# The inverse's working block and the state sum of a chunked scan, moved from SBUF to PSUM

## The chip, the cores and the metric

The kernel runs as one program on one core of a Trainium2 chip. The metric is the device time of one execution in microseconds (us). Three runs of the kernel before took 4306.79, 4306.83 and 4312.45 us; their median is 4306.83 us. The engines are named as in the profile: PE is the tensor engine (PEld its weight loads), DVE the vector engine, ACT the scalar engine, POOL the GpSimd engine, SP the engine that issues most of the DMAs.

## The reference

The model has two layers over 1024 latent tokens with 256 context tokens ahead of them, width 1024, in float32. Layer 0 mixes tokens with attention and a convolution; layer 1 mixes them with a bidirectional RWKV-7 scan; each layer ends in a SwiGLU feed-forward block. The change lies in the scan of layer 1:

```python
def step(S, inp):
    w_t, k_t, v_t, kk_t, b_t = inp[:5]
    sa = jnp.einsum('bhvk,bhk->bhv', S, kk_t)
    S = S * w_t[:, :, None, :] - sa[..., None] * b_t[:, :, None, :] + v_t[..., None] * k_t[:, :, None, :]
    y = jnp.einsum('bhvk,bhk->bhv', S, inp[5]) if emit else None
    return S, y
```

It runs for 16 heads of 64 features, forward and backward, first over the context and then, from the state so reached, over the latent tokens.

## The kernel before

**Stages.** The program goes through layer 0, the projections of layer 1, the scan (`layer1_scan`, lines 987 to 1407), and then the output projection and the feed-forward block of layer 1, which is nearly all matmuls. The scan lies between about 2400 and 3430 us of the span.

**The scan by chunks.** Tokens are cut into chunks of 64. The heads are done in four quarters `Q` of four heads, and each quarter in five scan steps `g` (the context, then four windows of 256 tokens), so there are 20 scan steps. A scan step handles both directions at once, four chunks each. Inside a chunk the recurrence is a triangular system, and its inverse is worked out ahead, on the chip. Four generators make up the work of a scan step, and the loop at the end of `layer1_scan` advances them in turn: `scan` of step n, `prep_inv` and `prep_mat` of step n+1, `prep_in` of step n+2.

**The inverse (`prep_inv`).** The 32 by 32 diagonal blocks lie in `A` with one half block per partition; `X` (128 partitions by 32 rows by 16 columns, 2 KB per partition) starts as a constant pattern `xid` and becomes the inverse by forward substitution. For each of 31 rows `k` there are two DVE instructions: line 1203 multiplies a column of `A` by row `k` of `X` into `tmp`, line 1204 subtracts `tmp` from the remaining rows of `X`. With n = 31-k rows and a width of k//2+1, the 31 rows hold 2856 elements per partition. Then `X` is transposed twice on DVE (lines 1207 and 1209, into `xd` and `xt`), ACT copies the result into `xc` (line 1214), and PE forms the off-diagonal block in two rounds of 32 small matmuls each per half (lines 1221 and 1228), each round into a PSUM tile `gp` that ACT reads out (lines 1224 and 1230). Both `gp` tiles come from the PSUM pool `pg`, which has one buffer of one bank (2 KB per partition) under the tag "g".

**The scan of a chunk (`scan`).** PE adds the values' part and the old state's part into `px` (lines 1263 and 1265), ACT copies it (1267), PE applies the inverse (1270, `pu`), ACT copies it (1272), PE forms the state's increment `ps` (line 1277, `pss` in the profile), DVE adds the old state `sc` (line 1284, `t` in the profile) and multiplies by the decay (line 1286, the new `sc`). `px`, `pu` and `pss` of a direction share one PSUM bank, under the tag c0 or c1, so each of them waits until the one before it has been read. POOL does the elementwise products of the preparation, all through line 1056 (`pmul`).

**Order.** The kernel is written in a tile framework, which places the waits and decides, with a timing model of its own, the fixed order of the instructions on each engine. [...] A tile's buffer is taken again only when all readers and writers of the tile that had it are done.

Of the kernel before, what the change touches and what calls it, by code (L numbers as in the profile page):

```python
# [9 lines left out]
F32 = mybir.dt.float32  # L10
F32R = mybir.dt.float32r
AF = mybir.ActivationFunctionType
# [31 lines left out]
class Kern:  # L44
# [7 lines left out]
    # ---------------------------------------------------------------- helpers  # L52
# [10 lines left out]
    def load_w(self, src, k=KB, m=P):  # L63
        """weight block (k*128 rows, m columns of DRAM) -> exact high and low parts"""
        raw = (self.Wr or self.W).tile([P, KB, P], F32, tag="raw", name="raw", bufs=self.wraw)
        if self.Wr:
            self.next_w()
        hi = self.W.tile([P, KB, P], F32R, tag="whi", name="whi", bufs=self.wbuf)
        lo = self.W.tile([P, KB, P], F32R, tag="wlo", name="wlo", bufs=self.wbuf)
        r, h, l = raw[:, :k, :m], hi[:, :k, :m], lo[:, :k, :m]  # L70
        self.nc.sync.dma_start(r, src.rearrange("(k p) m -> p k m", p=P))
        self.split(h, l, r)
        return h, l

    def load_w_rows(self, src):
        """128 rows by up to 1024 columns -> high and low parts"""
        n = src.shape[1]
        raw = (self.Wr or self.W).tile([P, KB, P], F32, tag="raw", name="raw", bufs=self.wraw)
        if self.Wr:
            self.next_w()  # L80
        hi = self.W.tile([P, KB, P], F32R, tag="whi", name="whi", bufs=self.wbuf)
        lo = self.W.tile([P, KB, P], F32R, tag="wlo", name="wlo", bufs=self.wbuf)
        fl = lambda t: t.rearrange("p a b -> p (a b)")[:, :n]
        self.nc.sync.dma_start(fl(raw), src)
        self.split(fl(hi), fl(lo), fl(raw))
        return fl(hi), fl(lo)

    # -------------------------------------------------------------- constants
# [19 lines left out]
    def params(self, *groups):  # L108
        """small parameters, a block of 128 features per column"""
# [40 lines left out]
    def ada(self, l, g0, g1, pool, bufs, psA, psT):  # L150
        """modulation of layer l for both condition vectors, groups g0..g1 of 1024 features: one step per weight block"""
        nc = self.nc
        for g in range(g0, g1):
            pa = psA.tile([P, 512], F32, tag="o", name="ada")[:, :256]
            for kb in range(KB):
                raw = pool.tile([P, D], F32, tag="araw", name="araw", bufs=bufs)
                nc.sync.dma_start(raw, self.I["ada_w"][l][kb * P:(kb + 1) * P, g * D:(g + 1) * D])
                for j in range(4):
                    nc.tensor.matmul(pa[32 * j:32 * j + 32], self.silc[:, kb], raw[:, 256 * j:256 * j + 256], start=kb == 0, stop=kb == KB - 1)
                if kb == KB - 1:  # L160
                    rows = pool.tile([P, 256], F32, tag="adr", name="adr", bufs=1)
                    nc.vector.tensor_copy(rows, pa)
                    pt = psT.tile([P, 512], F32, tag="o" if psA is psT else "m", name="adt")
                    for q in range(2):
                        nc.tensor.transpose(pt[:, q * P:(q + 1) * P], rows[:, q * P:(q + 1) * P], self.ident)
                    o = self.mod[l][:, g * 8:g * 8 + 8].rearrange("p (j q) s -> p j q s", q=2)
                    b = self.par["ada_b"][:, l * 48 + g * 8:l * 48 + g * 8 + 8].rearrange("p (j q) -> p j q", q=2)
                    nc.vector.tensor_tensor(o, pt[:, 0:256].rearrange("p (q j x) -> p j q x", q=2, j=4)[:, :, :, 0:2],
                                            b[:, :, :, None].to_broadcast([P, 4, 2, 2]), op=ALU.add)
                yield  # L170
# [8 lines left out]
    def rstd_bcast(self, src, n, scale, eps, pool, psum, tag="nn", bufs=3):  # L179
        """1/sqrt(scale * (sums of src over its blocks and their rows) + eps), on every partition: PSUM [P, n]"""  # L180
# [15 lines left out]
    def norm_mod(self, h, l, which, pool, psum):  # L196
        """h [P, 8, n] -> generator of (token range, fb, t, shift) with t = h * gain * rstd"""
# [26 lines left out]
    def load_hT(self, t0, n, dst, pool, psum, xb=4):  # L224
        """tokens t0..t0+n of the input streams, transposed: dst [P, 8, n]"""
# [17 lines left out]
    # ------------------------------------------------------- layer 0: mixer  # L243
    def layer0_mix(self):
# [6 lines left out]
        with ExitStack() as st:  # L251
# [96 lines left out]
            def conv(j, c=0, n=L - 30):  # L348
                """depthwise convolution of channel block j from column c on, to DRAM"""
# [8 lines left out]
            def conv2(j, cs):  # L358
                """the same, with the products and the sums on the other engines"""
# [17 lines left out]
            with tc.tile_pool(name="T1", bufs=1, side="right", reuse_waits="tile") as tp:  # L377
# [28 lines left out]
                # rotated keys, the same for all heads, by token  # L406
# [17 lines left out]
            # rotations with the gains of the rotated features; gains of the others, by feature  # L424
# [29 lines left out]
            def pair(p, wp, wn):  # L454
                """queries, keys (by token, normalised and rotated) and values of heads 2p and 2p+1"""
# [57 lines left out]
            # what is done with first lies where the residual stream comes next  # L513
            E = pool(left, name="AE", bufs=1)
            N = pool(left, name="AT", bufs=1)
            # what ends first lies where the loads of the next phase come
            N2 = pool(left, name="AH", bufs=1)
            vts[1] = values(N, 1)
            # queries and keys by feature, with a row for the maximum
# [6 lines left out]
            def head(i):  # L526
                """queries and keys of a head by feature"""
# [16 lines left out]
            def maxima(i):  # L544
                """maxima of the scores, as one more feature of the queries"""
# [19 lines left out]
            def attend(i):  # L565
# [3 lines left out]
                for t0, n in TT[1:] + TT[:1]:  # L569
# [16 lines left out]
                    # the other half of the rows holds the sums, the same in every row  # L586
# [15 lines left out]
            def conv_norm(t0):  # L602
                """layer norm over the channels, up to the shift, of 256 tokens, in place in DRAM"""
# [17 lines left out]
            def spread(gen, n, a, b):  # L621
                """n steps of gen between steps a and b of the attention of a head"""
                return [gen, n, a, b, 0]
# [39 lines left out]
    def layer0_out(self, hT, xh, xl, psum, tp):  # L663
        """the mixer's output projection; and the normalised input of the ffn"""
# [15 lines left out]
    def mix_out(self, l, wsrc, hT, xh, xl, passes, kbs, psum, rest, early=()):  # L680
        """residual stream plus gated projection; then the normalised input of the ffn, but for the last pass"""
        nc = self.nc
        self.gains(l, 1)
        # passes of (block of features, token tiles); the early ones have their weights, and most products, already
# [32 lines left out]
    # ------------------------------------------------------------------- ffn  # L717
# [46 lines left out]
    # ------------------------------------------------- layer 1: projections  # L764
    def layer1_proj(self, hT, close_h, LR):
# [8 lines left out]
        # lora features by direction, high parts in the direction's own rows, low parts in the others  # L774
# [8 lines left out]
        with ExitStack() as st:  # L783
# [10 lines left out]
            # heads of a feature block: sums over them, and back to their features  # L794
# [21 lines left out]
            def next_w():  # L816
                """the weight blocks rotate through two pools"""
# [4 lines left out]
            def mixed(o, i, fb, t0, n=256):  # L822
                """token mix i of feature block fb"""
# [162 lines left out]
    # ------------------------------------------------- layer 1: chunked scan  # L986
    def layer1_scan(self, R, prepared):
# [5 lines left out]
        with ExitStack() as st:  # L993
# [8 lines left out]
            # constants  # L1002
# [23 lines left out]
            # which keys a query sees, by token of the key: removal keys (lower rows) and keys (upper rows)  # L1026
# [17 lines left out]
            # tiles with parts that stay  # L1044
# [32 lines left out]
            def prep_in(Q, q, g, n):  # L1077
                """decayed keys and queries of the chunks of scan step g (both directions)"""
# [3 lines left out]
                for d, u in enumerate(units):  # L1082
# [21 lines left out]
                    # running sum of sigmoid(decay) in each chunk; products of decays and their inverses  # L1104
# [31 lines left out]
                for d, u in enumerate(units):  # L1136
                    # products of the removal keys with their queries, and the 32 by 32 diagonal blocks
# [20 lines left out]
            def prep_mat(Q, q, g, units):  # L1158
                """products of the chunks' keys with their queries, and the keys by token"""
# [32 lines left out]
            def prep_inv(units, par):  # L1192
                """inverses of the triangular systems of the chunks, transposed"""
                dt = units[0].dt
                # inverses of the diagonal blocks: one block per partition, its columns shared by two
                X = S.tile([P, 32, 16], F32, tag="X", name="X", bufs=1)
                nc.gpsimd.tensor_scalar(X, xid, 1.0, 0.0, op0=ALU.mult, op1=ALU.add)
# [12 lines left out]
                # inverses of the 64 by 64 blocks, transposed  # L1210
# [26 lines left out]
            def load_v(Q, tok, d):  # L1237
                """values of two chunks, in the upper rows"""
# [11 lines left out]
            def scan(Q, q, g, units):  # L1250
                lat = g > 0
                for j in range(4):
                    for d in range(2):
# [19 lines left out]
                        if not (g == 4 and j == 3):  # L1273
# [9 lines left out]
                            t1 = U.tile([P, 2, 64], F32, tag=f"t1{d}", name="t1", bufs=2)  # L1283
                            nc.vector.tensor_tensor(t1, ps, sc, op=ALU.add)
                            scn = U.tile([P, 2, 64], F32, tag=f"sc{d}", name="sc", bufs=3)
                            nc.vector.tensor_tensor(scn, t1, u.pc[:, :, m:m + 1].to_broadcast([P, 2, 64]), op=ALU.mult)
# [122 lines left out]
    def layer1_in(self, xh, xl, tp):  # L1409
        """the mixer's output, but for the last quarter of the features"""  # L1410
# [26 lines left out]
    # --------------------------------------------------------------------- all  # L1437
    def run(self):
        tc = self.tc
        pool = lambda s, **k: s.enter_context(tc.tile_pool(reuse_waits="tile", **k))  # L1440
        with ExitStack() as st:
# [12 lines left out]
            def phase(l, sizes, x, out):  # L1454
                """output projection of a mixer and the ffn after it; residual stream in hT"""
# [114 lines left out]
```

## Time and profile before

| | |
|---|---|
| median of three runs | 4306.83 us |
| span of the profiled execution, first to last instruction | 4304.2 us |
| PE busy | 3881.8 us (90%) |
| DVE busy | 2617.4 us (61%) |
| ACT busy | 1728.2 us (40%) |
| POOL busy | 1167.9 us (27%) |
| lines 1203 and 1204 together, DVE | 541.7 us in 1240 instructions |

A row of the profile names the line, the engine, the operation, the tiles (output <- inputs), the shapes and the count; behind the bar stand the total busy time in us and the mean of one instruction in ns, and then the time for which the engine idled just before them, with what ended most of it. A row of the timeline begins with the start in us and the length in us. A row of busy time by window gives the window, its length, and then for each engine the busy time and the number of instructions, and after those the granted clock of PE as a share of full speed, the share of the DMA engines and GB/s.

### The profile page before, as it was taken

The page shows a single profiled execution, that of the slowest core. Times are in us where ns is not written, and L with a number is a line of the kernel's source. Part 1 is how long each engine was busy: PE and PEld are TensorE (multiplying, and loading weights), DVE is VectorE, ACT ScalarE, POOL GpSimd, SP SyncE. Part 2 cuts the span into 40 slices and gives each one's busy share as a digit, 9 for nine tenths or more (in the row PEclk, how much of TensorE's full clock was granted, in tenths as well). Part 3 has the DMA queues.
Part 4 walks back from the last instruction along what each step waited for, and adds up shares of the span by engine and source line. Part 5 has one row for each costly group of instructions (what it writes and reads, how often), then busy time and mean ns, then how long its engine had stood idle before and what let it go on. Part 6 is the DMA issues. An engine that isn't in the chain of part 4 may idle for free. (4 is left out here: it accounts for less than half of the span.)

```text
span 4304.2 us, 70559 instructions
## 1 busy us (share of the span) xinstructions
PE 3881.8 (90%) x28764; PEld 3171.4 (74%) x28764; DVE 2617.4 (61%) x4577; ACT 1728.2 (40%) x3568; POOL 1167.9 (27%) x998
## 2 busy tenths in 40 slices
PE   8887999899999999979999578777877899999999
PEld 5665666688888888868779556666665778888887
DVE  5698676554343333366775798998899754333333
ACT  4436666632111111145665355556555533111111
POOL 3869455310000000042231443445344210000000
PEclk9898999899999999989999878787887899999999
DMA  4422221421111111022322211222222141111111
GB/s 169 138 68 74 85 85 61 152 69 45 35 40 40 40 40 40 30 79 69 112 89 87 75 56 49 73 67 64 70 65 63 52 126 59 49 49 47 42 49 59
DMA packets 301668, 297.06 MB, mean 69 GB/s; under 512 B 19408, under 2 KB 267872, under 8 KB 301344
## 3 DMA queue, kind: packets, MB, share of 16 engines
q1 hardware_dynamic: 293488, 277.07, 20.5%
q10 hardware_dynamic: 7056, 14.75, 1.0%
q8 instruction: 227, 3.72, 0.4%
q0 software_dynamic: 800, 0.73, 0.1%
q14 instruction: 97, 0.79, 0.1%
HBM read 246.36 MB, written 46.14 MB: 68 GB/s over the span
## 5 line engine op out<-in xcount | busy, mean ns | idle before, releaser
L59 PE MATMUL pf<-xh,whi 128*128 128x512 f32 (+1 forms) x1760 | 654.4, 372 | 0.0
L61 PE MATMUL pf<-xh,wlo 128*128 128x512 f32 (+1 forms) x1760 | 654.2, 372 | 0.0
L60 PE MATMUL pf<-xl,whi 128*128 128x512 f32 (+1 forms) x1760 | 654.0, 372 | 0.0
L54 ACT ACTIVATE whi<-raw 128x1024 fp32r<-128x1024 f32 (+1 forms) x207 | 214.8, 1048 | 905.3 <-PE pf L60 788.6
L762 DVE SCALAR_TENSOR_TENSOR hT<-pf,mod,hT 128x512 f32<-128x512 f32 (+1 forms) x440 | 306.0, 697 | 196.5 <-PE pf L61 194.5
L55 DVE TENSOR_TENSOR wlo<-raw,whi 128x1024 fp32r<-128x1024 f32 (+1 forms) x207 | 268.9, 1309 | 254.1 <-ACT whi L54 249.1
L751 DVE TENSOR_TENSOR sl<-sl,pf 128x512 f32<-128x512 f32 (+1 forms) x110 | 69.7, 634 | 580.9 <-PE pf L61 580.9
L60 PEld LDWEIGHTS pf<-xl,whi 128*128 128x128 f32 x1760 | 331.0, 188 | 64.6
L59 PEld LDWEIGHTS pf<-xh,whi 128*128 128x128 f32 x1760 | 330.9, 188 | 64.7 <-ACT xh L221 0.3
L61 PEld LDWEIGHTS pf<-xh,wlo 128*128 128x128 f32 x1760 | 330.8, 188 | 64.5
L60 PE MATMUL pf<-gl,whi 128*128 128x512 f32 (+1 forms) x880 | 324.1, 368 | 0.0
L61 PE MATMUL pf<-gh,wlo 128*128 128x512 f32 (+1 forms) x880 | 323.9, 368 | 0.0
L59 PE MATMUL pf<-gh,whi 128*128 128x512 f32 (+1 forms) x880 | 323.9, 368 | 0.0
L1204 DVE TENSOR_TENSOR X<-X,tmp 128x126 f32<-128x126 f32 (+22 forms) x620 | 274.3, 442 | 13.3
L581 POOL TENSOR_TENSOR pl<-pe,pt 128x512 fp32r<-128x512 f32 (+1 forms) x176 | 226.9, 1300 | 190.2 <-PE po L60 104.8
L1203 DVE TENSOR_TENSOR tmp<-A,X 128x126 f32<-128x126 f32 (+22 forms) x620 | 267.4, 431 | 13.3
L791 POOL MEMSET apad<- 128x8 f32 x4 | 0.2, 122 | 884.7 <-PE pf L61 884.7
L367 POOL TENSOR_TENSOR co<-co,cpr 128x655 f32<-128x655 f32 x90 | 193.7, 2153 | 46.0 <-ACT cpr L366 36.7
L54 ACT ACTIVATE gh<-sl 128x512 fp32r<-128x512 f32 (+1 forms) x110 | 64.9, 590 | 307.5 <-DVE sl L751 307.5
L59 PEld LDWEIGHTS pf<-gh,whi 128*128 128x128 f32 x880 | 165.9, 189 | 27.8
L60 PEld LDWEIGHTS pf<-gl,whi 128*128 128x128 f32 x880 | 165.9, 189 | 27.7
L61 PEld LDWEIGHTS pf<-gh,wlo 128*128 128x128 f32 x880 | 165.9, 189 | 27.7
(407 smaller groups left out, 9763.9 us busy)
## 6 DMA issues: line engine op xcount, KB each, us to landing
raw<-in_ffn_w_dram SPq DMA_DIRECT2D x132, 512.0 KB, 3.8
araw<-in_ada_w_dram SPq DMA_DIRECT2D x96, 512.0 KB, 4.4
low<-lod SPq DMA_DIRECT2D x40, 256.0 KB, 2.7
kw<-kd SPq DMA_DIRECT2D x40, 256.0 KB, 2.8
kkw<-kkd SPq DMA_DIRECT2D x40, 256.0 KB, 2.8
sv<-vd SPq DMA_DIRECT2D x80, 128.0 KB, 2.9
raw<-in_even_w_out_dram SPq DMA_DIRECT2D x16, 512.0 KB, 3.7
rw<-rd SPq DMA_DIRECT2D x32, 256.0 KB, 3.0
```

Of the source, the lines that this page charges most:

```text
L54: self.nc.scalar.activation(hi, src, AF.Copy)
L55: return self.nc.vector.tensor_tensor(lo, src, f32(hi), op=ALU.subtract)
L59: mm(ps, wh, xh, start=start, stop=False)
L60: mm(ps, wh, xl, start=False, stop=False)
L61: mm(ps, wl, xh, start=False, stop=stop)
L367: nc.gpsimd.tensor_tensor(co, co, pr, op=ALU.add)
L581: nc.gpsimd.tensor_tensor(pl, pe, f32(pt), op=ALU.subtract)
L751: nc.vector.tensor_tensor(sl[:, :n], sl[:, :n], pp[1][:, :n], op=ALU.mult)
L762: nc.vector.scalar_tensor_tensor(hT[ti][:, mb], ps[:, :n], g[:, mb], hT[ti][:, mb], op0=ALU.mult, op1=ALU.add)
L791: nc.gpsimd.memset(ap[:, :, c:c + 1], 0.0)
L1203: nc.vector.tensor_tensor(tmp, A[:, k + 1:32, k:k + 1].to_broadcast([P, n, wd]), X[:, k:k + 1, 0:wd].to_broadcast([P, n, wd]), op=ALU.mult)
L1204: nc.vector.tensor_tensor(X[:, k + 1:32, 0:wd], X[:, k + 1:32, 0:wd], tmp, op=ALU.subtract)
```

## The change

The tile `X` is taken from the PSUM pool `pg` instead of the SBUF pool `S`. It has the tag "g" there, and so the one buffer that the two `gp` tiles use. [...] In the chunk's state update the sum is written back into its PSUM tile `ps` instead of the SBUF tile `t1`, and the product with the decay reads it from there. Comments and docstrings are removed as well, and empty lines stand in their place, so that the line numbers up to line 1282 stay.

```diff
             def prep_inv(units, par):
                 dt = units[0].dt
-                X = S.tile([P, 32, 16], F32, tag="X", name="X", bufs=1)
-                nc.gpsimd.tensor_scalar(X, xid, 1.0, 0.0, op0=ALU.mult, op1=ALU.add)
+                X = pg.tile([P, 32, 16], F32, tag="g", name="X")
+                nc.scalar.activation(X, xid, AF.Copy)
                 A = S.tile([P, 32, 32], F32, tag="A", name="A")
...
-                            t1 = U.tile([P, 2, 64], F32, tag=f"t1{d}", name="t1", bufs=2)
-                            nc.vector.tensor_tensor(t1, ps, sc, op=ALU.add)
+                            nc.vector.tensor_tensor(ps, ps, sc, op=ALU.add)
                             scn = U.tile([P, 2, 64], F32, tag=f"sc{d}", name="sc", bufs=3)
-                            nc.vector.tensor_tensor(scn, t1, u.pc[:, :, m:m + 1].to_broadcast([P, 2, 64]), op=ALU.mult)
+                            nc.vector.tensor_tensor(scn, ps, u.pc[:, :, m:m + 1].to_broadcast([P, 2, 64]), op=ALU.mult)
                             cur[d] = (svn, scn)
```

## The prediction

> **What bounds the kernel now.** I read the page's busy slices first, to see which stages there are, then the busy time by window, then the groups of the scan's stage.
>
> ```profile
> span 4304.2 us, 70559 instructions
> PE   8887999899999999979999578777877899999999
> DVE  5698676554343333366775798998899754333333
> 3550.00:4304.00 754.00, 745.44 (x3255) 604.68 (x3254) 286.30 (x372) 137.32 (x188) 4.25 (x3) 0.99 0.16 51
> 2416.00:3409.00 993.00, 752.95 (x11792) 622.64 (x11791) 898.30 (x1998) 541.89 (x1426) 435.00 (x408) 0.82 0.20 60
> ```
>
> After 3550 us PE sets the time (745 of 754 us). In the stage of the change, from the first substitution at 2416 us to the last at 3409 us, the roles are turned: DVE is busy for 898 of 993 us, PE for 753, at a granted clock of 0.82. So what the change does to DVE there can move the end; the PE stage after it keeps its length.
>
> What fills DVE is the substitution: 541.7 of 898 us, in 1240 instructions. But their lengths don't follow their sizes:
>
> ```profile
> L1204 DVE TENSOR_TENSOR X<-X,tmp 128x126 f32<-128x126 f32 (+22 forms) x620 | 274.3, 442 | 13.3
> L1203 DVE TENSOR_TENSOR tmp<-A,X 128x126 f32<-128x126 f32 (+22 forms) x620 | 267.4, 431 | 13.3
> L1203 DVE TENSOR_TENSOR tmp<-A,X 128x45 f32<-128x45 f32 x20 | 4.1, 203 | 0.4
> L1204 DVE TENSOR_TENSOR X<-X,tmp 128x128 f32<-128x128 f32 x20 | 5.7, 284 | 0.3
> L1203 DVE TENSOR_TENSOR tmp<-A,X 128x100 f32<-128x100 f32 x20 | 16.0, 798 | 0.5
> ```
>
> 128 elements take 284 ns, 100 elements 798 ns on the mean. The timeline shows why. First DVE and then POOL over the same 6 us, then DVE alone at a place where POOL does nothing:
>
> ```profile
> 2917.31 1.28 DVE L1286 TENSOR_TENSOR sc<-t,pcw 128x128 f32<-128x128 f32 x1
> 2918.52 0.28 DVE L1284 TENSOR_TENSOR t<-pss,sc 128x128 f32<-128x128 f32 x1
> 2918.72 1.11 DVE L1203 TENSOR_TENSOR tmp<-A,X 128x110 f32<-128x110 f32 x1
> ...
> 2919.95 1.35 DVE L1204 TENSOR_TENSOR X<-X,tmp 128x110 f32<-128x110 f32 x1
> ```
> ```profile
> 2917.20 2.50 POOL L1056 TENSOR_TENSOR qa<-pp,kkw 64x512 f32<-64x512 f32 x2
> 2919.78 1.39 POOL L1056 TENSOR_TENSOR kp<-kkw,pi 128x512 f32<-128x512 f32 x1
> ```
> ```profile
> 3400.36 0.26 DVE L1204 TENSOR_TENSOR X<-X,tmp 128x110 f32<-128x110 f32 x1
> 3400.66 0.27 DVE L1203 TENSOR_TENSOR tmp<-A,X 128x108 f32<-128x108 f32 x1
> 3400.00:3425.00 25.00, 23.26 (x456) 18.87 (x452) 17.62 (x55) 18.27 (x44) 0.00 (x0) 0.93 0.21 65
> ```
>
> Lines 1203 and 1204 with 110 elements take 1.11 and 1.35 us while a POOL product runs, 0.26 us while none does (108 elements: 0.27). The delayed instructions end about when a POOL product ends (2919.70, 2921.17). Each has both inputs in SBUF. Line 1284, with one input in PSUM, sits in the middle of POOL's 2.50 us and takes 0.28 us. So I read the excess as waiting for POOL, and only of instructions with two SBUF inputs.
>
> **The change part by part.**
>
> *Substitution, X in PSUM.* Lines 1203 and 1204 keep one SBUF input each, as line 1284 has. The price without waiting, from the 45 and 128 element groups above: (284-203)/83 = 0.98 ns per element, 159 ns fixed. A block has 62 instructions and 2 x 2856 elements: 62 x 159 + 5712 x 0.976 = 15.4 us, against 541.7/20 = 27.1 us now. Over 20 blocks DVE loses 541.7 - 309 = 233 us of work.
>
> *What a PSUM operand costs.* For reading there are rows:
>
> ```profile
> L1284 DVE TENSOR_TENSOR t<-pss,sc 128x128 f32<-128x128 f32 x143 | 39.8, 281 | 12.8 <-PE pss L1277 12.4
> L1286 DVE TENSOR_TENSOR sc<-t,pcw 128x128 f32<-128x128 f32 x143 | 56.8, 400 | 0.2
> L1175 DVE TENSOR_TENSOR l<-kps,msk 128x512 f32<-128x512 f32 x128 | 86.9, 680 | 18.7 <-PE kps L1174 18.1
> L762 DVE SCALAR_TENSOR_TENSOR hT<-pf,mod,hT 128x512 f32<-128x512 f32 x352 | 263.8, 750 | 178.6 <-PE pf L61 176.6
> ```
>
> With PSUM read, 128 elements take 281 ns, without it 284: nothing. [...]
>
> No DVE instruction writes PSUM in this trace. Bounds by the nearest rows: above, the widest spread of two forms that read 512 elements from PSUM, 750 - 680 = 70 ns; below, 281 - 284 = -3 ns. I take zero, since the read costs zero; 70 ns on line 1204 would be 31 x 0.07 = 2.2 us per block.
>
> *State update.* Line 1286 loses its second SBUF input: 400 to 281 ns over 152 instructions (160 chunks and directions, less the last chunk of each quarter's two), 18 us. Line 1284 now writes PSUM (bounds as above, at most 11 us). The bank is held until 1286 has read it, so line 1263 of the next chunk waits for 1286, not 1284. Line 1265, right behind it, waits for 1286 already; so at most the 0.3 us of a group of four matmuls is lost per chunk and direction, at least nothing. I take nothing: 1286 also ends sooner.
>
> *The start of X.* POOL loses 20 instructions and a wait, ACT gets 20 copies of 512 elements, priced by its own copy of that size, 623 ns, 12 us in all (ACT is busy for 542 of 993 us); writing PSUM there is unseen too, and what is queued behind is a chunk's `xs` and `sv` copies.
>
> ```profile
> L1319 ACT ACTIVATE gsq<-yw 128x512 f32<-128x512 f32 x12 | 7.5, 623 | 19.7 <-DVE yw L1317 19.7
> POOL X L1197 <- DVE xd L1207: 94.2, 16, 19.2
> ```
>
> *The bank.* This is the cost. `X` shares one buffer with the `gp` tiles, so block n+1 can't start before line 1230 of block n has read the last `gp`. Today it starts earlier: the row of line 1203 below begins a new block 8.8 us before that read ends.
>
> ```profile
> 2902.49 1.04 DVE L1207 STREAM_TRANSPOSE xd<-X 128x512 f32<-128x512 f32 x1
> ...
> 2906.97 0.21 DVE L1203 TENSOR_TENSOR tmp<-A,X 128x31 f32<-128x31 f32 x1
> 2914.60 1.19 ACT L1230 ACTIVATE xc<-gp 32x512 f32<-32x512 f32 x2
> 2902.49:2915.80 13.31, 12.66 (x215) 10.85 (x214) 10.18 (x27) 10.60 (x25) 2.47 (x3) 0.67 0.12 40
> 2902.49:2915.80 13.31, 3.95 (x17) 0.67 0.12 40
> L1207 DVE STREAM_TRANSPOSE xd<-X x20: 987/1036/1071, 2454.6 to 3408.4; 128x512 f32<-128x512 f32 x20
> ```
>
> The tail from `xd` to that read is 13.3 us here, a usual one. The second window row counts only lines 1203 and 1204. The blocks come every (3408.4 - 2454.6)/19 = 50.2 us.
>
> *The sum.* The new loop of a block: 15.4 us of substitution; 62 gaps of 0.04 us between dependent instructions (start to start 0.30 us for 0.26 above), 2.5; the tail, 13.3; the copy into `X`, 0.6; and DVE's other work that falls among the substitution. That other work is (898.3 - 541.7)/20 = 17.8 us a block; 2.1 are the two transposes of `X` (2 x 1.04) and (10.18 - 3.95) - 2.1 = 4.2 fit in the tail, as they do above, which leaves 11.6. Together 43.4 us against 50.2: 6.8 x 19 = 129 us. The first block runs nearly alone:
>
> ```profile
> 2416.00:2455.00 39.00, 31.04 (x62) 0.67 0.17 51
> ```
>
> It gives 31.0 - 15.4 = 15.6 us. In all 145 us off the span of 4304.2; the median lies 2.6 us above the span, so 4306.8 - 145 = 4162 us.
>
> PE allows this. Its waits for DVE that the change can shorten:
>
> ```profile
> PE px L1263 <- DVE t L1284: 60.3, 35, 8.1
> PE tps L1179 <- DVE l L1175: 45.9, 18, 6.5
> PE kps L1174 <- DVE l L1175: 27.4, 22, 4.1
> PE abp L1142 <- DVE kb L1134: 25.8, 10, 10.5
> PE px L1265 <- DVE sc L1286: 22.1, 26, 3.5
> ```
>
> They sum to 181 us, and the forecast needs 145 of them. That the tile framework will put the instructions in another order can't be priced from the trace; it widens the range.
>
> **The rivals.**
>
> *All of the relief arrives.* If DVE alone sets the stage and the framework fills the tail with other work, all 233 + 18 = 251 us go: 4056 us; with PE's clock unchanged only the 181 us of its waits, 4125. For it: DVE is the only engine above 80%. Against it: PE is at 753 of 993 us, the loop is new, and PE's clock would have to rise (0.82 here, 0.99 where PE is 99% busy).
>
> *PSUM is dear.* Every instruction on `X` takes the 70 ns more of the upper bound: 62 x 0.07 = 4.3 us, a loop of 47.7 us, 2.5 x 19 + 15.6 - 4.3 = 59 us off, 4248 us. Against it: 281 ns to 284 ns; for it, only that writing is unseen. [...]
>
> *Slower: the tail grows.* With `X` behind the last `gp`, PE and ACT set when DVE may go on, and in the row above PE is 95% busy in the tail. From a tail of 13.3 + 6.8 = 20.1 us on, the loop is longer than today's. The longest tail of the 20 is 22.1 us:
>
> ```profile
> 2763.10 1.04 DVE L1207 STREAM_TRANSPOSE xd<-X 128x512 f32<-128x512 f32 x1
> 2784.02 1.19 ACT L1230 ACTIVATE xc<-gp 32x512 f32<-32x512 f32 x2 [5.32 <-PE gp L1228]
> ```
>
> With all tails so long: 8.8 - 6.8 = 2.0 us x 19 - 15.6 = 22 us slower, 4329 us. Against it: it is the extreme of 20, and the rest of the queue gets emptier.
>
> *The change doesn't do what it says:* the waiting for POOL stays. Then the loop is 27.1 + 2.5 + 11.6 + 13.3 + 0.6 = 55.1 us, 4.9 x 19 = 93 us slower, 4400 us. Against it: line 1284's 0.28 us amid POOL's work.
>
> **How the numbers follow.** Forecast, a saving of 90 to 205 us: 0.64. All of it: 0.13. Dear PSUM or another small saving: 0.12. No change: 0.03. Long tails 0.05, lock unchanged 0.03. So faster 0.89, same 0.03, slower 0.08, where a measurement tells 0.2% (8.6 us) from no change. The range, 4075 to 4265 us, takes in most of the full relief and the dear PSUM, and leaves out both slower cases.
>
> **What would show it.** In the profile after: lines 1203 and 1204 at 0.17 to 0.30 us whatever POOL does, 310 us in sum (right; 390 would be dear PSUM, 540 an unchanged lock); line 1286 near 281 ns; the period of line 1207 near 43 us; DVE waiting for ACT's copy into `X`; PE's waits for DVE far below 181 us and its clock above 0.82. The forecast is wrong if line 1204 is much longer than 1203 at the same size, or if the period stays near 50 us.

## The result and the profile after

The changed kernel takes 4181.72 us (median of four runs, 4180.5 to 4188.13) beside 4306.9 us for the kernel before: a ratio of 0.9705, 95% interval 0.9693 to 0.9717, or 125 us less. The forecast was 4162 us.

The page of the changed kernel, then busy time by window from the first substitution to the last (all instructions, then lines 1203 and 1204 alone), then the groups of that stage. In the changed kernel line 1283 is the sum and line 1285 the product with the decay (1284 and 1286 before).

```profile
span 4186.4 us, 70705 instructions
2424.00:3289.00 865.00, 706.29 (x11927) 587.13 (x11928) 694.08 (x2020) 561.71 (x1466) 434.09 (x391) 0.88 0.24 69
2424.00:3289.00 865.00, 313.71 (x1240) 0.88 0.24 69
L1204 DVE TENSOR_TENSOR X<-X,tmp 128x126 f32<-128x126 f32 (+22 forms) x620 | 159.7, 258 | 13.9
L1203 DVE TENSOR_TENSOR tmp<-A,X 128x126 f32<-128x126 f32 (+22 forms) x620 | 154.0, 248 | 52.3 <-ACT X L1197 38.6
L1283 DVE TENSOR_TENSOR pss<-pss,sc 128x128 f32<-128x128 f32 x147 | 42.6, 291 | 8.6 <-PE pss L1277 6.8 <-ACT sv L1272 0.9
L1285 DVE TENSOR_TENSOR sc<-pss,pcw 128x128 f32<-128x128 f32 x146 | 40.5, 281 | 0.0
L1207 DVE STREAM_TRANSPOSE xd<-X x20: 660/696/725, 2450.4 to 3288.0; 128x512 f32<-128x512 f32 x20
L1203 DVE TENSOR_TENSOR tmp<-A,X x620: 157/256/297, 2424.3 to 3287.6; 128x126 f32<-128x126 f32 x15, 128x30 f32<-128x30 f32 x10, 128x78 f32<-128x78 f32 x10, 128x110 f32<-128x110 f32 x10
```

The same view of line 1203 in the kernel before:

```profile
L1203 DVE TENSOR_TENSOR tmp<-A,X x620: 151/274/2359, 2416.2 to 3407.5; 128x126 f32<-128x126 f32 x15, 128x30 f32<-128x30 f32 x10, 128x78 f32<-128x78 f32 x10, 128x110 f32<-128x110 f32 x10
```

(the three times are the shortest, the median and the longest, in ns). The substitution falls from 541.7 to 313.7 us of DVE, and the longest of the 620 instructions of line 1203 takes 297 ns, POOL or not, where it took 2359. DVE is busy for 694 of 865 us (80%) where it was 898 of 993 (90%); PE's granted clock there rises from 0.82 to 0.88. The blocks come every (3288.0 - 2450.4)/19 = 44.1 us instead of 50.2.

The stage from the first line 1203 to the last `xd` took 3408.4 - 2416.2 = 992.2 us and takes 3288.0 - 2424.3 = 863.7 us: 128.5 us less. What follows it takes 898.4 instead of 895.8 us, so 126 us are left, about the 125 us between the medians. The two spans differ by less, 117.8 us, because the profiled execution after is the slowest of its four (4188.13 us): it was late before any changed instruction ran. The first product of the feed-forward block of layer 0, before and then after, shows it, at 978.4 and 986.7 us:

```profile
L751 DVE TENSOR_TENSOR sl<-sl,pf x110: 413/687/690, 978.4 to 4265.9; 128x512 f32<-128x512 f32 x88, 128x256 f32<-128x256 f32 x22
```
```profile
L751 DVE TENSOR_TENSOR sl<-sl,pf x110: 410/687/690, 986.7 to 4147.8; 128x512 f32<-128x512 f32 x88, 128x256 f32<-128x256 f32 x22
```

The loop through the shared bank can be read from the timeline of the changed kernel, ACT first and then DVE:

```profile
2806.46 1.19 ACT L1224 ACTIVATE gz<-gp 32x512 f32<-32x512 f32 x2
...
2810.08 1.19 ACT L1230 ACTIVATE xc<-gp 32x512 f32<-32x512 f32 x2
2811.30 0.60 ACT L1197 ACTIVATE X<-xid 128x512 f32<-128x512 f32 x1
```
```profile
2799.91 0.70 DVE L1207 STREAM_TRANSPOSE xd<-X 128x512 f32<-128x512 f32 x1
...
2809.80 0.69 DVE L1175 TENSOR_TENSOR l<-kps,msk 128x512 f32<-128x512 f32 x1 [4.02 <-PE kps L1174]
2811.93 0.20 DVE L1203 TENSOR_TENSOR tmp<-A,X 128x31 f32<-128x31 f32 x1 [1.44 <-ACT X L1197]
```

`X` is started directly behind the read of the last `gp` (2811.27), and the next substitution directly behind that; DVE idles for 1.44 us before it. The waits of the stage:

```profile
DVE l L1175 <- PE kps L1174: 60.4, 40, 6.1
DVE tmp L1203 <- ACT X L1197: 38.6, 12, 8.4
PE gp L1221 <- DVE xd L1207: 22.3, 9, 8.5
PE abp L1142 <- DVE kb L1134: 17.0, 9, 6.6
PE kps L1174 <- DVE l L1175: 15.4, 20, 2.2
PE px L1263 <- DVE sc L1285: 7.4, 9, 2.3
PE tps L1179 <- DVE l L1175: 6.0, 9, 1.4
```

PE's waits for DVE that summed to 181 us have fallen to about 46 (the last four rows; none is listed in front of line 1265), but PE waits longer for `xd` in front of line 1221 (22.3 us; 5.6 before). New is DVE's 38.6 us behind the copy into `X`.

### The profile page after: what moved, and what is told of

It is laid out like the page before. It is cut to its first block, busy times and chain, and to the rows that moved or that the text cites. A ratio compares the mean times of both kernels' runs of the same rounds, so it can differ in the third digit from the quotient of the medians.

```text
span 4186.4 us, 70705 instructions
## 1 busy us (share of the span) xinstructions
PE 3832.1 (92%) x28764; PEld 3132.3 (75%) x28764; DVE 2403.9 (57%) x4577; ACT 1741.1 (42%) x3590; POOL 1161.3 (28%) x978
## 5 line engine op out<-in xcount | busy, mean ns | idle before, releaser
L60 PEld LDWEIGHTS pf<-gl,whi 128*128 128x128 f32 x880 | 165.9, 189 | 27.7
L1203 DVE TENSOR_TENSOR tmp<-A,X 128x126 f32<-128x126 f32 (+22 forms) x620 | 154.0, 248 | 52.3 <-ACT X L1197 38.6
L354 DVE SCALAR_TENSOR_TENSOR co<-yp,parC,co 128x1310 f32<-128x1310 f32 (+1 forms) x90 | 177.0, 1967 | 1.5
```

The lines of the kernel that those rows point to most:

```text
L60: mm(ps, wh, xl, start=False, stop=False)
L354: nc.vector.scalar_tensor_tensor(co, yp[:, w + c:w + c + n], cw(j, w), co, op0=ALU.mult, op1=ALU.add)
L1203: nc.vector.tensor_tensor(tmp, A[:, k + 1:32, k:k + 1].to_broadcast([P, n, wd]), X[:, k:k + 1, 0:wd].to_broadcast([P, n, wd]), op=ALU.mult)
```

## The experiments

The theory: a DVE instruction with two SBUF inputs waits while POOL reads SBUF (1.11 and 1.35 us beside a product in the trace of before, 0.26 us without one), the move to PSUM takes that wait away, and the shared bank takes a part of the gain back. The rivals: the state sum brings the gain; any POOL work would do the same, or PSUM is quicker in itself; PE sets the period by now. Each number has its kernel before on the same chip, so the ratios are compared.

**Is it POOL's reading?** The kernel before, each of POOL's products in the scan replaced by three memsets (the products are left out):

```diff
-                nc.gpsimd.tensor_tensor(o, a, b, op=ALU.mult)
+                for _ in range(3):
+                    nc.gpsimd.memset(o, 0.01)
```

> The kernel before with X in SBUF, but each product on POOL replaced by three memsets of its output, so that POOL is about as busy but reads nothing; the products are left out of the computation. Theory (a DVE instruction with two SBUF inputs waits for a POOL instruction that reads SBUF): lines 1203 and 1204 fall to 300 to 340 us in sum, a few waits being left behind POOL's scalar instruction of line 1105, and the time to 4060 to 4160 us. Rival (any work of POOL on SBUF delays them): they stay above 450 us in sum and the time above 4230 us.

Measured: 4125.32 us, ratio 0.9564 (0.9542 to 0.9586). The groups of this kernel and a window from its first substitution to its last, whose lines behind the edit are one higher (1204 and 1205 are the substitution, 1287 the state's product):

```profile
L1205 DVE TENSOR_TENSOR X<-X,tmp 128x126 f32<-128x126 f32 (+22 forms) x620 | 161.6, 261 | 13.9
L1204 DVE TENSOR_TENSOR tmp<-A,X 128x126 f32<-128x126 f32 (+22 forms) x620 | 158.0, 255 | 15.0 <-POOL X L1198 1.1
L1287 DVE TENSOR_TENSOR sc<-t,pcw 128x128 f32<-128x128 f32 x152 | 42.9, 287 | 0.3
2435.00:3229.00 794.00, 689.16 (x11734) 569.65 (x11734) 645.41 (x1992) 543.11 (x1425) 481.49 (x993) 0.91 0.19 57
```

With `X` in SBUF the substitution takes 319.6 us instead of 541.7, though POOL is busier than ever (481 of 794 us; 435 of 993 before). What POOL writes delays next to nothing; what it reads does: the two lines take 255 and 261 ns a piece here, against 431 and 442 before.

The single records say the same, sorted by what POOL ran at the same time. Before, 898 of the 1240 instructions of lines 1203 and 1204 have no POOL instruction beside them; they take 249 ns on the mean and 301 at most, and the 268 that have nothing but products beside them take 956. In `pool_writes` 781 have nothing but memsets beside them and 437 nothing at all, and both take 253 ns. The 22 that meet POOL's scalar instruction of line 1106, which reads SBUF, take 527, though it is about as short as a memset (638 against 523 ns). In the kernel after, 427 have nothing but products beside them and take 237 ns, 308 at most.

**Does the move gain anything else?** The same replacement in the changed kernel:

> The changed kernel with each POOL product replaced by three memsets of its output, as in pool_writes; the products are left out of the computation. Theory (the change gains by nothing but the missing wait for POOL's reads, and pays for it with the shared bank): without those reads there is nothing to gain, and the bank's price is left, so it is 15 to 45 us slower than pool_writes (0.9564 of before, 4125 us). Rival (operands in PSUM are quicker in themselves, or the start of X on ACT frees POOL): not slower than pool_writes.

Measured: 4187.68 us, ratio 0.9716 (0.9701 to 0.9731): 0.0152 above `pool_writes`, some 65 us. Without POOL's products the change is a loss, so its gain hangs on the missing wait for them. The loss is larger than the 15 to 45 us expected.

**Is the loss the bank?** As before, with the `gp` tiles in the two-buffer pool of the key products, so that `X` has its bank for itself:

```diff
-                gp = pg.tile([P, 16, 32], F32, tag="g", name="gp")
+                gp = pk.tile([P, 16, 32], F32, tag="k", name="gp")
...
-                gp = pg.tile([P, 16, 32], F32, tag="g", name="gp2")
+                gp = pk.tile([P, 16, 32], F32, tag="k", name="gp2")
```

> x_bank_k (X alone in its bank, gp in the pool of the key products) with each POOL product replaced by three memsets of its output; the products are left out of the computation. Theory (the 62 us by which pool_writes_after, 4187.7, lies above pool_writes, 4125.3, are the shared bank): with a bank of its own it comes back to pool_writes, 4105 to 4140 us. Rival (PSUM operands or the start on ACT cost something in themselves once POOL is out of the way): it stays above 4160 us.

Measured: 4128.97 us, ratio 0.9573 (0.956 to 0.9586), the same as `pool_writes` within some 11 us. So the loss is the shared bank.

**What the bank costs the changed kernel.** First with `gp` in the pool of the projections (`pz`, tag "z"), then in that of the key products (the diff above), both with POOL's products as they are:

> As the changed kernel, but the two gp tiles come from the two-buffer PSUM pool of the projections and diagonal blocks, so that X has the bank for itself. Theory (the loop through the shared bank sets the period of 44.1 us; DVE waits 38.6 us for the copy into X): the wait falls below 10 us, the period to 41 to 42.5 us, the time to about 4140 us. Rival 1 (PE sets the period by now): within 8 us of 4181.7. Rival 2 (the two-buffer pool becomes the new wait, since its tiles now queue behind gp): above 4190 us.

> As x_own_bank, but the gp tiles come from the two-buffer pool of the key products instead of that of the projections. Theory: X is free of the loop here as well, 4125 to 4160 us; which pool is better depends on where PE's waits are, and x_own_bank shows few for either. Rival (the key products, which DVE reads one after the other, get delayed behind gp): above 4160 us, with more waiting in front of lines 1174 and 1179.

Measured: 4143.91 us, ratio 0.9611 (0.9595 to 0.9628), and 4133.75 us, ratio 0.9588 (0.9571 to 0.9605). The second, its transposes, its groups and its window:

```profile
L1207 DVE STREAM_TRANSPOSE xd<-X x20: 668/712/718, 2439.7 to 3229.6; 128x512 f32<-128x512 f32 x20
L1203 DVE TENSOR_TENSOR tmp<-A,X 128x126 f32<-128x126 f32 (+22 forms) x620 | 153.5, 248 | 13.7 <-ACT X L1197 0.3
2416.00:3237.00 821.00, 701.71 (x11918) 583.28 (x11920) 691.08 (x2002) 552.77 (x1451) 431.20 (x389) 0.89 0.25 72
```

DVE's wait for the copy into `X` is gone (0.3 us of 38.6), the period is (3229.6 - 2439.7)/19 = 41.6 us, and both kernels beat the changed one, by 0.0094 and 0.0117 of before, 40 and 50 us. So PE does not set the period of the changed kernel. It is near it now: 702 of 821 us busy.

With one `gp` tile in each of the two pools:

> X alone in its bank; the first gp tile in the pool of the projections, the second in that of the key products, so that each pool gets one more tile a step instead of two. Theory (the bank of its own is what counts, and the pools are alike): 4125 to 4145 us, ratio 0.957 to 0.962 to before. Rival (two tiles in one pool held its own tiles up): below 4125 us.

Measured: 4141.76 us, ratio 0.9609 (0.9596 to 0.9622). The three kernels with a bank for `X` can't be told apart with certainty; the pool matters little.

**Half of the way.** Only the second `gp` in the pool of the projections, so that `X` waits for the read of the first (line 1224 instead of 1230):

> As the changed kernel, but only the second gp tile comes from the two-buffer pool of the projections; X then waits for the read of the first gp, about 4 to 5 us before the read of the second. Theory (the length of the loop through the bank sets the period): a part of the 38 us that a bank of its own brought, 4145 to 4168 us, DVE's wait for the copy into X between 5 and 30 us. Rival (only full independence counts): above 4170 us. Rival 2 (fewer tiles queue in the two-buffer pool, and this outweighs): below 4140 us.

Measured: 4182.77 us, ratio 0.9704 (0.9688 to 0.9721): no gain over the changed kernel. Its waits:

```profile
PE gp L1221 <- DVE xd L1207: 30.3, 10, 15.6
DVE tmp L1203 <- ACT X L1197: 27.7, 12, 6.5
```

DVE's wait fell by 11 us only, and PE's wait for `xd` rose by 8 (22.3 in the changed kernel). The order of the instructions is another one, as the start of the second and of the last block shows, for this kernel and then for the changed one:

```profile
2474.67 0.19 DVE L1203 TENSOR_TENSOR tmp<-A,X 128x31 f32<-128x31 f32 x1
...
3251.09 0.20 DVE L1203 TENSOR_TENSOR tmp<-A,X 128x31 f32<-128x31 f32 x1 [0.95 <-ACT X L1197]
```
```profile
2463.41 0.20 DVE L1203 TENSOR_TENSOR tmp<-A,X 128x31 f32<-128x31 f32 x1 [5.22 <-ACT X L1197]
...
3258.95 0.20 DVE L1203 TENSOR_TENSOR tmp<-A,X 128x31 f32<-128x31 f32 x1 [2.86 <-ACT X L1197]
```

From the second block to the last the blocks come every (3251.09 - 2474.67)/18 = 43.1 us, against 44.2 in the changed kernel. But the first block began at 2419.72, and so the second follows it by 55.0 us, against 39.1 (from 2424.29). The small gain per block is lost there. `x_bank_zk` has a second block almost as late (53.7 us), but from there on its blocks come every 40.7 us, and it is 41 us quicker. Why a wait that ends 4 to 5 us earlier shortens the period by 1 us only is not settled. That the length of the loop alone sets the period falls with this run; that `X` must be free of `gp` stands.

**The parts.** `X` in PSUM with the sum left in SBUF, and the sum in PSUM with `X` left in SBUF:

> X in PSUM alone; the state sum stays in SBUF. Theory (the relief is the substitution's, and the sum adds the 18 us of line 1286's waiting at most): lines 1203 and 1204 sum to about 312 us, line 1286 stays near 400 ns, the time lies 5 to 20 us above the changed kernel's 4181.7, about 4192 us. Rival (the state sum sits on the chain from chunk to chunk, and its shorter line 1286 brings much of the gain): 4230 us or more.

> The state sum in PSUM alone; X stays in SBUF and its start on POOL. Theory: line 1286 falls from 400 to about 281 ns, lines 1203 and 1204 stay near 540 us in sum, the time is 5 to 18 us below before, about 4295 us. Rival (the PSUM bank held until the product has read it delays the next chunk's first matmuls): 4307 us or more, with PE's wait in front of line 1263 above 60 us.

Measured: 4212.09 us, ratio 0.9769 (0.9753 to 0.9785), and 4295.59 us, ratio 0.9966 (0.9956 to 0.9975). `X` alone brings 0.0231 of the 0.0295, the sum alone 0.0034; but on top of `X` the sum brings 0.0064, some 28 us. So `only_x` lies between its theory (4192 us) and its rival (4230 us), and `only_sum` where its theory put it. A row of `only_x` and one of the kernel after point to a reason, against 397 ns of line 1286 and 835 of line 1134 before:

```profile
L1286 DVE TENSOR_TENSOR sc<-t,pcw 128x128 f32<-128x128 f32 x152 | 70.0, 463 | 0.1
```
```profile
L1134 DVE SCALAR_TENSOR_TENSOR kb<-ar,kp 128x512 f32<-128x512 f32 x40 | 49.0, 1225 | 5.0 <-POOL kp L1056 3.8 <-PE tps L1179 0.9 <-PE kps L1174 0.4
```
```profile
L1134 DVE SCALAR_TENSOR_TENSOR kb<-ar,kp 128x512 f32<-128x512 f32 x40 | 33.4, 835 | 4.5 <-PE tps L1179 3.1 <-POOL kp L1056 1.3
```

(the last row is of the kernel before). With the substitution out of POOL's way, these two, which still have two SBUF inputs, are held more: 463 ns instead of 397, 1225 instead of 835. In `only_x` that makes line 1286 cost 152 x (463 - 281) = 27.7 us more than with its input in PSUM, which would be the 28 us. It is argued, not shown: DVE also waits longer for the copy into `X` there (60.2 us; 38.6 in the kernel after). And it is no rule for every instruction: in `only_sum`, with line 1286 out of the way, lines 1203 and 1204 stay at 427 and 432 ns.

**The start of X on ACT alone,** `X` staying in SBUF:

```diff
-                nc.gpsimd.tensor_scalar(X, xid, 1.0, 0.0, op0=ALU.mult, op1=ALU.add)
+                nc.scalar.activation(X, xid, AF.Copy)
```

> The kernel before with nothing but the start of X issued on ACT instead of POOL; X and the sum stay in SBUF. Theory: POOL loses a wait of 94 us that hides nothing, ACT gets 12 us that lie beside DVE's work: within 10 us of before. Rival (POOL's products come sooner and DVE's waits with them change place): more than 15 us either way.

Measured: 4291.88 us, ratio 0.9963 (0.9949 to 0.9977), some 16 us less (10 to 22): the rival's side, just. Two groups and a wait of this kernel:

```profile
L1204 DVE TENSOR_TENSOR X<-X,tmp 128x126 f32<-128x126 f32 (+22 forms) x620 | 275.4, 444 | 13.7
L1203 DVE TENSOR_TENSOR tmp<-A,X 128x126 f32<-128x126 f32 (+22 forms) x620 | 264.1, 426 | 12.7
ACT X L1197 <- DVE xd L1207: 50.9, 16, 13.3
```

The substitution is as long as before, so the gain is not there. POOL's products no longer stand in its queue behind the 94 us of waiting for `X`. That this is where the 16 us come from is argued, not shown.

## Why the prediction was right

**The mechanism** was read rightly: waiting for POOL, only of instructions with two SBUF inputs. The substitution was put at 309 us and takes 313.7; line 1286 at 281 ns and takes 281.

**The price of PSUM.** Taken as zero for reading, and that holds: line 1203 with `X` read from PSUM takes 248 ns, its twin with both inputs in SBUF and POOL not reading takes 255. Also taken as zero for writing, which the trace of before didn't show: it is 10 ns (line 1204 against 1203: 258 to 248; line 1283 against the sum into SBUF: 291 to 281), far from the bound of 70. With that the rival of a dear PSUM falls. The 390 us that the prediction names for a dear PSUM rest on a price per instruction that no run shows: the two lines sum to 313.7 us.

**The loop through the bank** was the right limit: before 12 of the 19 later blocks DVE waits for the copy into `X`, and with a bank of its own for `X` the period falls. Its period, 43.4 us, is 0.7 us off, and that it is so near is in part luck, as two terms were mis-sized against each other. The tail from `xd` to the last read of `gp` was taken as it was, 13.3 us; the one in the timeline above takes 2811.27 - 2799.91 = 11.4, and the mean of the 20 is 11.2 (14.7 before). DVE's other work was taken as 17.8 us a block; it is (694.1 - 313.7)/20 = 19.0. That term the prediction had as constant, but what still has two SBUF inputs is held longer: line 1134 alone went from 33.4 to 49.0 us. From the first line 1203 of a block to its `xd` it is 31.1 us on the mean where 29.5 were forecast (15.4 + 2.5 + 11.6), and from there to the next block 12.8 where 13.9 were.

**The first block** was put at 15.6 us less; it took 2454.6 - 2416.2 = 38.4 us to its `xd` and takes 2450.4 - 2424.3 = 26.1, which is 12.3. With the loop, (50.2 - 44.1) x 19 = 116 us instead of 129, and the 2.6 us lost behind the stage, these are 19 of the 20 us between forecast and result.

**PE** allowed it, but not by its waits alone, as the prediction had it. The four waits of the list fell by 135 us, but PE's idle time in the stage by 81 (from 993.0 - 753.0 = 240.0 to 865.0 - 706.3 = 158.7), since it waits elsewhere now. The other 47 us are its busy time, for no fewer matmuls (11927 in the window after, 11792 before), at a granted clock of 0.88 instead of 0.82.

**The start of X** was given a price on ACT (0.6 us a block) and no worth on POOL. By itself it brings 16 us, so something was left out; that it is POOL's lost wait of 94 us is not shown. What it is worth in the changed kernel, no run separates.

**The state sum** was put at 18 us of DVE's work, and left out of the loop's sum. Alone it brings 15 us, on top of `X` 28.

**The rivals.** All of the relief, 4056 us, did not arrive, and would not have even with a bank for `X`: 4134 us there, and 4125 with POOL's products replaced. An unchanged lock and a growing tail, the two slower ones, fall with the 313.7 us and the mean tail of 11.2 us.

## What to carry to other kernels

Where a short DVE instruction with two SBUF inputs takes several times its usual length (here 956 ns beside POOL's products, 249 with nothing beside it), look at what POOL reads at that moment: with one of the two inputs in PSUM it didn't wait here (237 ns beside the products), at 10 ns for a result that goes there too (258 to 248). The bank for it must not be one that a later step of the same chain needs, or the overlap of one block's end with the next one's start is paid for it: here 40 to 50 of some 170 us. And instructions left with two SBUF inputs can then wait longer (line 1134 here 1225 ns instead of 835), so the whole list of them should be read, not the costliest alone.

## What was not expected of the hardware

The 32 by 32 transposes of `X` (line 1207, 512 elements per partition) take 692 ns from PSUM and 1036 ns from SBUF. POOL has no part in it: in `pool_writes`, where its products are replaced, they take 1039 ns. The row of the kernel after, then of the one before:

```profile
L1207 DVE STREAM_TRANSPOSE xd<-X 128x512 f32<-128x512 f32 x20 | 13.8, 692 | 0.1
```
```profile
L1207 DVE STREAM_TRANSPOSE xd<-X 128x512 f32<-128x512 f32 x20 | 20.7, 1036 | 0.3
```

It is no effect of the place in the program: the second transpose, from SBUF to SBUF, stays at 1045 ns in the kernel after. Over 20 blocks it saves 7 us of DVE's work.

But it is not SBUF alone. These transposes read their input with a step of 16 elements (`p r c -> p c r`, and the second likewise). One in layer 0 that reads from SBUF without such a step, each element 32 times over, takes 704 ns for as many elements, on 64 partitions, and one from PSUM without a step takes 711:

```profile
L590 DVE STREAM_TRANSPOSE rt<-po 64x512 f32<-64x512 f32 x16 | 11.4, 711 | 7.1 <-PE po L61 6.7
L593 DVE STREAM_TRANSPOSE rt<-rr 64x512 f32<-64x512 f32 x16 | 11.3, 704 | 0.4
```

So the step seems to cost time in SBUF (1036 and 1045 ns against 704) and none in PSUM (692 against 711). No run here changes the step alone.
